# Denominators of the last pair of heads in the latent attention, summed on all 64 rows of a head and inverted without a transfer

## The chip, the cores and the metric

The kernel runs on one NeuronCore of one Trainium2 chip. Its engines work side by side, each through its own list of instructions in order: TensorE (PE) multiplies matrices and writes to PSUM, VectorE (DVE) and ScalarE (ACT) work element by element, GpSimd (POOL) does so too, and SyncE (SP) issues the transfers between DRAM and the on-chip memory SBUF. The metric is the device time of one execution in microseconds; the median of three runs counts.

## The reference, cut to what matters

Two layers of a diffusion trunk are computed for 128 context tokens and 1024 latent tokens. The second layer is a latent attention with 16 heads, each with a value of 64 columns. Latent tokens read all latent and all context keys (1152), context tokens only the context keys (128); the heads' output is multiplied by a gate and projected.

```python
def dense_attention(q, k, v, scale, sink=None):
    ...
            p = jax.nn.softmax(s, axis=-1)
        return jnp.einsum("bhgqk,bkhd->bqhgd", p.astype(v.dtype), v)

def mla_attend(q, k, v, g, w_out):
    b, L = q.shape[0], q.shape[1]
    out = dense_attention(q[:, :, :, None, :], k, v, MLA_SCALE)
    return (out.reshape(b, L, MLA_WIDTH) * jax.nn.silu(g)) @ w_out
...
        xl = xl + gate * out
    y_sample = rms_norm(xl, final_norm_w)
```

## The kernel before, in words

**Pairs and chunks.** The heads are taken in eight pairs (`pair_main`, j = 0 to 7). A pair keeps its values transposed: 128 partitions, 64 for each head, and the tokens along the row. Its tokens are worked in three chunks: latent tokens 0 to 511, latent tokens 512 to 1023, and the 128 context tokens. The last pair takes them in the order 0, context, 512.

**One chunk.** For every block of 128 keys and each of the two heads PE computes scores in three matmuls (`sc`, L1450 to L1452; operands are split into a high and a low part to keep the precision), ACT takes the exponential (L1457) into a tile `pf`, and PE multiplies the values by it into the accumulator `acco` (L1471), two key blocks at a time. A round is thus twelve score matmuls and then the value matmuls. The score buffers in PSUM are two; PE waits for the exponential that frees one. POOL adds the exponentials of all key blocks into `totals` (L1486), one tile for each head, with the keys along the partitions.

**Denominators.** `gather` runs when a chunk's values are complete. ACT copies `acco` to the pair's tile `op` (L1495). In `sums`, PE multiplies `totals` by a column of ones into `den` (L1502): one row for head 0, one for head 64 partitions further down. `store` lets ACT copy the two rows to SBUF (L1508), writes them to DRAM (`rd1_d`, shown as `rd_d`, L1509), and reads them back spread over 128 partitions, eight numbers each. `invert` takes the reciprocal on VectorE and writes it to DRAM (L1517). `fetch` loads the gate (`g1_d`, shown as `g_d`, L1523) and reads every head's reciprocals back, broadcast to its 64 partitions; their product is taken on VectorE. `gated` multiplies by `op` and stores the result to `o1_d` (shown as `o_d`, L1531). Calls made through a helper that keeps the program's order appear as L1272. `after(n, ...)` and `steps.behind(n, ...)` put these parts n steps later into the program's text.

**The output projection.** After the last pair, nine token tiles of 128 are projected. A tile's `o_d` columns of all eight pairs are loaded (L1654), so its load waits for the last pair's store of that chunk. ACT casts it to the high part, VectorE forms the low part (L249, L250, forms 128x1024), and PE runs 2 x 24 matmuls (L256 to L258) into two accumulators. VectorE multiplies an accumulator by the layer's gate (L1060), POOL adds it to the residual (L1061), then comes the final norm.

```python
            for q in range(2):
                acc = psum("mm", "acc")
                for k in range(KT):
                    mm3(acc, at[:, 0, k], at[:, 1, k], *wos[q, k], k == 0, k == KT - 1)
```

**What sets the order.** The framework orders each engine's instructions by a simulated timeline, within the dependencies and the orders that the program pins. Work of the projection therefore stands between score groups of the last chunk where the simulated timeline found its operand ready. The weights of the projection are loaded and split during the last pair.

Of the kernel before, what the change touches and what calls it, by code (L numbers as in the profile page):

```python
# [12 lines left out]
F32 = mybir.dt.float32  # L13
F32R = mybir.dt.float32r
AF = mybir.ActivationFunctionType
ALU = mybir.AluOpType
# [176 lines left out]
class Steps:  # L193
# [5 lines left out]
    def after(self, n, f, *a):  # L199
        self.due.setdefault(self.now + n, []).append(partial(f, *a))  # L200
# [20 lines left out]
def hybrid_trunk(ctx: ExitStack, tc: tile.TileContext, I, O, dbg=None, stage=99):  # L221
    nc = tc.nc
    pe, act, dve, pool, dma = nc.tensor, nc.scalar, nc.vector, nc.gpsimd, nc.sync
# [15 lines left out]
    def scratch(name, shape):  # L239
        return dr.tile(shape, F32, tag=name, name=name)  # L240

    def psum(tag, name):
        return ps.tile([128, 512], F32, tag=tag, name=name, bufs=2)
# [44 lines left out]
    g1_d = scratch("g1_d", [KT, 128, T])  # L288
    o1_d = scratch("o1_d", [KT, 128, T])
# [964 lines left out]
    p7, p7a = Space(mem), Space(mem, right=True)  # L1254
    AK, BK, AQ, BQ = [], [], [], []

    def operand_set():
# [5 lines left out]
        pool.memset(AK[i][96:97].bitcast(F32), 1.0)  # L1263
        dma.dma_start(AK[i][64:96].bitcast(F32), kp_d[0])
        dma.dma_start(BK[i][64:96].bitcast(F32), kp_d[1])
    ones = p7.tile([128, 1], F32, name="ones")
    pool.memset(ones, 1.0)
    steps = Steps()

    def pinned(f, *a):  # L1270

        tc.keep_in_program_order(f(*a))  # L1272
    after = steps.after
    either, taken = cycle(("mm", "tr")), []

    def spare(name):

        taken.append(steps.now)
        assert taken.count(steps.now) <= 4
        return psum(next(either), name)  # L1280
# [208 lines left out]

    ending = []  # L1490

    def gather(j, op, q0, n, acc, totals):

        qs = slice(q0, q0 + n)
        act.copy(op[:, qs], acc)  # L1495
        dn = p7.tile([128, 8], F32, tag="dn1", name="dn1", bufs=3)[:, 0:n // 64]
        flat = [rd1_d[2 * j + a, qs].rearrange("(p c) -> p c", p=64) for a in range(2)]

        def sums():
            den = spare("den")  # L1500
            for a in range(2):
                pe.matmul(den[a * 64:a * 64 + 1, 0:n], ones, totals[a], start=True, stop=True)  # L1502
            after(1, store, den)

        def store(den):
            row = p7.tile([65, 512], F32, tag="dr1", name="dr1", bufs=2)[:, 0:n]
            for a in range(2):
                act.copy(row[a * 64:a * 64 + 1], den[a * 64:a * 64 + 1, 0:n])  # L1508
                dma.dma_start(rd1_d[2 * j + a:2 * j + a + 1, qs], row[a * 64:a * 64 + 1])  # L1509
            for a in range(2):  # L1510
                after(2, pinned, dma.dma_start, dn[a * 64:(a + 1) * 64], flat[a])
            after(4, invert)

        def invert():
            pinned(dve.reciprocal, dn, dn)
            for a in range(2):
                dma.dma_start(flat[a], dn[a * 64:(a + 1) * 64])  # L1517
            after(2, fetch)

        def fetch():  # L1520
            gt = p7.tile([128, n], F32, tag=f"gt{n}", name="gt1")
            rb = p7.tile([128, n], F32, tag=f"rb{n}", name="rb1")
            dma.dma_start(gt, g1_d[j, :, qs])  # L1523
            for b in range(2):
                pinned(dma.dma_start, rb[b * 64:(b + 1) * 64], bcast_rows(rd1_d[2 * j + b, qs], 64))
            after(2, pinned, dve.tensor_tensor, gt, gt, rb, ALU.mult)
            after(3, gated, gt)

        def gated(gt):
            pinned((pool if ending else dve).tensor_tensor, gt, op[:, qs], gt, ALU.mult)  # L1530
            dma.dma_start(o1_d[j, :, qs], gt)  # L1531
        steps.behind(1, sums)

    wo1 = I["mla_w_out"][0]
# [69 lines left out]
    for pair in range(8):  # L1604
        op = p7.tile([128, T], F32, tag="op", name="op")
# [101 lines left out]
```

## Time and profile before

| | |
|---|---|
| median of three runs | 1846.62 us (1841.96 to 1848.19) |
| profiled execution, own time | 1853.15 us |
| its span, first to last instruction | 1851.1 us |
| mean granted TensorE clock | 0.955 |
| busy shares PE, DVE, ACT, POOL | 93%, 56%, 44%, 40% |
| last pair's denominators of chunk 0 done on PE | 1707.5 us |
| first matmul of the output projection | 1738.5 us |
| last matmul | 1842.8 us |

The profile is of one execution. Times in its rows are microseconds from the span's start, except the "mean ns of one" in groups. A row of the timeline is an instruction or several of one kind with the idle time of its engine before it and what ended that; a row of the chain is a piece of the chain of waits that ended last; a row of windows is a stretch with the busy time of each engine in it. Names such as `arenaF` are regions of SBUF from which the tiles are taken; `acc`, `sc`, `acco` and `den` are tiles in PSUM. What stands in "idle before" is time in which the engine waited; it costs something only where that engine sets the end.

### The profile page before, as it was taken

Reading aid. Unit: us, or ns where it says so; the run is one execution under the profiler, and the core shown is the slowest. Engines: PE = TensorE matmul, PEld = TensorE weight load, DVE = VectorE, ACT = ScalarE, POOL = GpSimd, SP = SyncE. Lnnn points to the kernel's source line nnn. Section 1 sums busy time; section 2 is a strip of 40 time slices with the busy share of each in tenths; the row PEclk is TensorE's granted clock in tenths of the full one; section 3 lists DMA queues with packets and bytes.
Section 4 is the critical chain, followed back from the end, with each engine's and each line's share of the span. In section 5 each row is a group of like instructions: output and inputs, shape, how many; then the busy total and the mean of one; then the engine's idle time right before and its main releaser. Section 6 shows DMA issues by size and latency. Waiting matters only on the chain.

```text
span 1851.1 us, 27076 instructions
## 1 busy us (share of the span) xinstructions
PE 1720.0 (93%) x9031; PEld 1322.7 (71%) x9031; DVE 1041.7 (56%) x1989; ACT 817.7 (44%) x1873; POOL 744.3 (40%) x741
## 2 busy tenths in 40 slices
PE   6899999999998888988999999999999999998898
PEld 3799999877775776666688898655665665654486
DVE  5665545655545467667765434655665665564243
ACT  5532323665655344444434322534535634545321
POOL 3510000133333344565624010556666665565432
PEclk9999999999998888898999999989999998999899
DMA  7423323444435697555553533010220121114342
GB/s 259 124 84 92 118 64 110 130 114 122 121 93 146 195 279 245 164 194 165 164 171 86 175 99 97 18 54 23 51 72 23 45 75 28 37 29 122 108 154 91
DMA packets 210655, 210.26 MB, mean 114 GB/s; under 512 B 36162, under 2 KB 175504, under 8 KB 210516
## 3 DMA queue, kind: packets, MB, share of 16 engines
q1 hardware_dynamic: 210372, 208.40, 37.7%
q8 instruction: 72, 1.18, 0.3%
q14 instruction: 67, 0.55, 0.1%
q0 software_dynamic: 144, 0.13, 0.0%
HBM read 151.94 MB, written 51.72 MB: 110 GB/s over the span
## 4 chain that ended last, share of the span: by engine, by line
PE 65%; DMA 12%; DVE 8%; POOL 4%; issue 3%; ACT 3%; SPq 2%; POOLq 0%; DVEq 0%; ACTq 0%
PE acc L256 12%; PE acc L258 12%; PE acc L257 12%; PE acco L1471 6%; PE pp L1429 3%; PE sc L1450 3%; DMA arenaG<-cum_d 3%; PE sc L1452 3%; PE sc L1451 3%; DVE arenaR L250 2%; DMA arenaF<-rd_d 2%; DMA rd_d<-arenaF 2%; PE st L808 1%; DMA arenaG<-rd_d 1%; PE den L1502 1%
## 5 line engine op out<-in xcount | busy, mean ns | idle before, releaser
L256 PE MATMUL acc<-arenaR 128*128 128x384 f32 (+4 forms) x1248 | 430.8, 346 | 25.5 <-ACT arenaR L249 10.4
L1486 POOL TENSOR_TENSOR arenaG<-arenaG 128x512 f32<-128x512 f32 x256 | 333.1, 1320 | 229.1 <-ACT arenaG L1457 202.0
L257 PE MATMUL acc<-arenaR 128*128 128x384 f32 (+3 forms) x1176 | 400.7, 341 | 0.1
L258 PE MATMUL acc<-arenaR 128*128 128x384 f32 (+4 forms) x1152 | 389.1, 339 | 0.2
L256 PEld LDWEIGHTS acc<-arenaR 128*128 128x128 f32 x1248 | 242.8, 195 | 69.0 <-issue 16.5
L1457 ACT ACTIVATE arenaG<-sc 128x512 f32<-128x512 f32 (+1 forms) x304 | 174.6, 580 | 218.9 <-PE sc L1452 210.9
L209 DVE TENSOR_REDUCE arenaF<-pp 128x1 f32<-128x384 f32 (+1 forms) x400 | 199.2, 539 | 110.0 <-PE pp L1429 108.6
L257 PEld LDWEIGHTS acc<-arenaR 128*128 128x128 f32 x1176 | 228.5, 194 | 15.8 <-issue 3.6
L258 PEld LDWEIGHTS acc<-arenaR 128*128 128x128 f32 x1152 | 224.0, 194 | 16.6 <-issue 2.2
L250 DVE TENSOR_TENSOR arenaR<-arenaF,arenaR 128x512 fp32r<-128x512 f32 (+2 forms) x144 | 129.7, 914 | 71.8 <-ACT arenaR L249 65.6
L249 ACT CAST arenaR<-arenaF 128x512 fp32r<-128x512 f32 (+3 forms) x160 | 101.1, 648 | 142.9 <-DMA arenaF<-in_ab_w_in_dram 24.0
L1471 PE MATMUL acco<-arenaG 128*64 128x512 f32 (+1 forms) x608 | 150.4, 609 | 0.0
L1005 ACT ACTIVATE arenaG<-arenaG,arenaF 128x128 f32<-128x128 f32 x288 | 88.4, 389 | 116.2 <-POOL arenaG L1003 115.8
L749 POOL TENSOR_TENSOR arenaG<-arenaF,arenaG 128x512 fp32r<-128x512 f32 x28 | 48.1, 1716 | 149.4 <-PE acco L753 85.6
L1429 PE MATMUL pp<-arenaR 96*128 96x384 f32 (+1 forms) x300 | 92.4, 363 | 11.6 <-DVE arenaF L209 11.1
L1450 PE MATMUL sc<-arenaR 96*128 96x512 f32 (+1 forms) x228 | 94.5, 414 | 5.5 <-ACT arenaG L1457 5.2
L1429 PEld LDWEIGHTS pp<-arenaR 96*128 96x128 f32 x300 | 55.1, 192 | 55.4 <-DVE arenaF L209 25.0
L258 PE MATMUL acc<-arenaR,arenaS 128*128 128x512 f32 (+1 forms) x240 | 91.5, 386 | 0.0
L1452 PE MATMUL sc<-arenaR 97*128 97x512 f32 (+1 forms) x228 | 89.6, 396 | 0.0
L1451 PE MATMUL sc<-arenaR 96*128 96x512 f32 (+1 forms) x228 | 89.5, 393 | 0.0
L1003 POOL TENSOR_SCALAR_AFFINE_SELECT arenaG<-arenaG 128x512 f32<-128x512 f32 x72 | 60.5, 862 | 66.4 <-DMA arenaG<-cum_d 53.9
L1471 PEld LDWEIGHTS acco<-arenaG 128*64 128x64 f32 x608 | 36.8, 140 | 70.3 <-issue 67.9
(328 smaller groups left out, 3342.8 us busy)
## 6 DMA issues: line engine op xcount, KB each, us to landing
arenaF<-in_ada_w_dram SPq DMA_DIRECT2D x96, 256.0 KB
arenaG<-cum_d SPq DMA_DIRECT2D x36, 512.0 KB
arenaF<-in_ab_w_in_dram SPq DMA_DIRECT2D x51, 256.0 KB
z_d<-arenaF SPq DMA_DIRECT2D x36, 128.0 KB
xs_d<-arenaF SPq DMA_DIRECT2D x8, 576.0 KB
arenaF<-xs_d SPq DMA_DIRECT2D x9, 512.0 KB
arenaF<-z_d SPq DMA_DIRECT2D x9, 512.0 KB
x_d<-arenaG SPq DMA_DIRECT2D x9, 512.0 KB
```

Of the source, the lines that this page charges most:

```text
L209: f()
L250: lo_eng.tensor_tensor(lo, src, hi.bitcast(F32), ALU.subtract)
L256: pe.matmul(out, ah, bh, start=first, stop=False)
L257: pe.matmul(out, ah, bl, start=False, stop=False)
L258: pe.matmul(out, al, bh, start=False, stop=last)
L1429: pe.matmul(pp[:, 0:w], AQ[s][0:96, t * 128:(t + 1) * 128], AK[s][0:96, k0:k0 + w], start=True, stop=True)
L1450: pe.matmul(sc[:, 0:n], AK[s][0:96, ks], BQ[s][:, qs], start=True, stop=False)
L1451: pe.matmul(sc[:, 0:n], BK[s][:, ks], AQ[s][0:96, qs], start=False, stop=False)
L1452: pe.matmul(sc[:, 0:n], AK[s][:, ks], AQ[s][:, qs], start=False, stop=True)
L1457: act.activation(pf, sc[:, 0:n], AF.Exp, scale=SCALE_M)
L1471: put = lambda: pe.matmul(acc[0][a * 64:(a + 1) * 64], V[:, a], pfs[a], start=(i < 2 and k < 2), stop=(last and k >= len(todo) - 2))
L1486: pool.tensor_tensor(totals[a], first[a] if i == 1 else totals[a], pfs[a], ALU.add)
```

## The change

For the last pair alone (j = 7), `gather` hands over to `gather_last`. The tile of ones becomes 64 columns wide, so that the matmul writes the denominator to all 64 rows of its head at once. VectorE takes the reciprocal of that PSUM tile, 128 x n numbers, into SBUF. The gate is loaded early and multiplied by `op`, then by the reciprocal, both on VectorE, and the product is stored. Copies of the rows on ACT and the way through `rd1_d` fall away for this pair: eight transfers in each of the three chunks. The other seven pairs keep their way and use one column of the ones.

```diff
-    ones = p7.tile([128, 1], F32, name="ones")
+    ones = p7.tile([128, 64], F32, name="ones")
...
+    def gather_last(j, op, q0, n, totals):
+
+        qs = slice(q0, q0 + n)
+        gt = p7.tile([128, n], F32, tag=f"gt{n}", name="gt1")
+        rb = p7.tile([128, n], F32, tag=f"rb{n}", name="rb1")
+        dma.dma_start(gt, g1_d[j, :, qs])
+
+        def sums():
+            den = spare("den")
+            for a in range(2):
+                pe.matmul(den[a * 64:(a + 1) * 64, 0:n], ones, totals[a], start=True, stop=True)
+            dve.tensor_tensor(gt, op[:, qs], gt, ALU.mult)
+            after(1, divided, den)
+
+        def divided(den):
+            dve.reciprocal(rb, den[:, 0:n])
+            dve.tensor_tensor(gt, gt, rb, ALU.mult)
+            dma.dma_start(o1_d[j, :, qs], gt)
+        steps.behind(1, sums)
+
     def gather(j, op, q0, n, acc, totals):
 
         qs = slice(q0, q0 + n)
         act.copy(op[:, qs], acc)
+        if j == 7:
+            return gather_last(j, op, q0, n, totals)
...
-                pe.matmul(den[a * 64:a * 64 + 1, 0:n], ones, totals[a], start=True, stop=True)
+                pe.matmul(den[a * 64:a * 64 + 1, 0:n], ones[:, 0:1], totals[a], start=True, stop=True)
```

The framework's order moves with it. On PE, in the last chunk of the last pair, the first matmuls of the output projection (`acc`) stood behind all scores:

```order
L1450 MATMUL sc<-arenaS,arenaR 128x512
L1451 MATMUL sc<-arenaS,arenaR 128x512
L1452 MATMUL sc<-arenaS,arenaR 128x512
L1471 MATMUL acco<-arenaG 64x512 x4
L256 MATMUL acc<-arenaR 128x512
L257 MATMUL acc<-arenaR 128x512
```

With the change they stand in the third of the four rounds, behind nine of its twelve score matmuls:

```order
L1450 MATMUL sc<-arenaR 128x512
L1451 MATMUL sc<-arenaR 128x512
L1452 MATMUL sc<-arenaR 128x512
L256 MATMUL acc<-arenaR 128x512
L257 MATMUL acc<-arenaR 128x512
...
L1450 MATMUL sc<-arenaS,arenaR 128x512
L1451 MATMUL sc<-arenaS,arenaR 128x512
L1452 MATMUL sc<-arenaS,arenaR 128x512
L1471 MATMUL acco<-arenaG 64x512 x4
```

Four projection matmuls moved ahead of fifteen scores, and most of tile 0's others follow between the remaining score groups.

On ACT, from the copy of the context chunk's accumulator on, the exponentials (L1457) and the casts of the first projection tiles (128x1024) stood thus:

```order
L1495 COPY arenaF<-acco 128x128
L1508 COPY arenaF<-den 1x512 x2
L1508 COPY arenaF<-den 1x128 x2
L1457 ACTIVATE arenaG<-sc 128x512 x15
L249 CAST arenaR<-arenaF 128x1024
L1457 ACTIVATE arenaG<-sc 128x512
L249 CAST arenaR<-arenaF 128x1024
```

Now:

```order
L1515 COPY arenaF<-acco 128x128
L1457 ACTIVATE arenaG<-sc 128x512 x9
L249 CAST arenaR<-arenaF 128x1024
L1457 ACTIVATE arenaG<-sc 128x512 x4
L249 CAST arenaR<-arenaF 128x1024
L1457 ACTIVATE arenaG<-sc 128x512
L249 CAST arenaR<-arenaF 128x1024
```

The four copies of denominators are gone, and the first cast stands ahead of seven exponentials instead of one.

On VectorE the reciprocals of the context chunk and of chunk 0 now stand like this, between the splits of weights (128x512) and of projection tiles (128x1024):

```order
L250 TENSOR_TENSOR arenaR<-arenaF,arenaR 128x512
L1503 TENSOR_TENSOR arenaF<-arenaF 128x512
...
L1507 RECIPROCAL arenaF<-den 128x128
L1507 RECIPROCAL arenaF<-den 128x512
L1503 TENSOR_TENSOR arenaF<-arenaF 128x128
L1508 TENSOR_TENSOR arenaF<-arenaF 128x512
L1508 TENSOR_TENSOR arenaF<-arenaF 128x128
L250 TENSOR_TENSOR arenaR<-arenaF,arenaR 128x1024 x2
```

The small reciprocal goes first and the product that is stored for chunk 0 (L1508, 128x512) is the fourth instruction behind the weights. (Of L1503 to L1515 the numbers are the changed kernel's.)

## The prediction

> **What bounds the kernel now.** I read the page first, then the end of the program by windows, then the PE timeline of the gap found there, then the chain of waits through it.
>
> The page's first part, all engines over the span:
>
> ```profile
> PE 1720.0 (93%) x9031; PEld 1322.7 (71%) x9031; DVE 1041.7 (56%) x1989; ACT 817.7 (44%) x1873; POOL 744.3 (40%) x741
> ```
>
> PE is the bound, so the change is worth what it takes out of PE's lost time, and it touches only the last pair (from about 1700 us on). Windows there; the columns are busy time by engine, then the granted clock (PEclk), the DMA share and GB/s:
>
> ```profile
> 1708.00:1712.00 4.00, 2.38 (x7) 1.37 (x8) 1.03 (x2) 3.89 (x10) 0.42 (x1) 0.96 0.50 114
> 1712.00:1716.00 4.00, 4.00 (x12) 1.92 (x12) 0.00 (x0) 1.19 (x2) 4.00 (x4) 0.61 0.46 172
> 1732.00:1736.00 4.00, 0.19 (x2) 0.00 (x0) 0.14 (x1) 0.00 (x0) 1.25 (x1) 0.95 0.62 177
> 1736.00:1740.00 4.00, 1.53 (x4) 1.16 (x4) 1.23 (x1) 1.92 (x3) 0.94 (x1) 0.50 1.07 338
> 1740.00:1744.00 4.00, 4.00 (x13) 1.66 (x12) 1.23 (x1) 1.25 (x2) 0.82 (x1) 0.70 0.83 255
> ...
> 1760.00:1780.00 20.00, 20.00 (x90) 16.55 (x89) 8.44 (x9) 4.30 (x6) 8.16 (x10) 1.00 0.62 197
> ```
>
> PE loses time twice, near 1710 and at 1732 to 1738, and behind each loss it runs about 4 us at a reduced clock. From 1760 on it is full at clock 1.00. The PE timeline says what it waited for (idle time and releaser in brackets):
>
> ```profile
> 1711.55 0.69 PE L1450 MATMUL sc<-arenaR 96*128 96x512 f32 x1 [1.42 <-ACT arenaG L1457]
> ...
> 1738.47 0.79 PE L256 MATMUL acc<-arenaR 128*128 128x512 f32 x1 [6.28 <-ACT arenaR L249]
> ...
> 1755.86 0.50 PE L256 MATMUL acc<-arenaR 128*128 128x512 f32 x1 [0.84 <-DVE arenaF L1060]
> ```
>
> The 6.28 us is the first matmul of the output projection waiting for its operand. The chain of waits shows where that comes from (start, us, what; pieces in between left out):
>
> ```profile
> 1706.35 1.18 PE den L1502 x4
> ...
> 1709.74 0.43 ACT arenaF L1508
> 1710.17 4.49 DMA rd_d<-arenaF
> ...
> 1715.22 1.89 DMA arenaF<-rd_d
> ...
> 1721.53 3.70 DMA rd_d<-arenaF
> ...
> 1725.75 4.02 DMA arenaF<-rd_d
> 1729.87 1.00 DVE arenaF L1272
> ...
> 1733.03 4.32 DMA arenaF<-o_d
> 1737.37 1.05 ACT arenaR L249
> ```
>
> From the denominators' end (1706.35 + 1.18 = 1707.53) to the cast's end (1738.42) are 30.9 us. All up to the product at 1729.87 is the denominators' way through DRAM and back: four hops and the waits between them.
>
> **The change part by part.** The sum is made against the profiled execution (1853.15 us, span 1851.1); its gain in us is then taken off the median of the three runs (1846.62), which lies 6.5 us lower.
>
> *Removed on ACT.* Four copies of denominator rows stood ahead of the exponentials:
>
> ```profile
> 1709.15 1.73 ACT L1508 COPY arenaF<-den 1x512 f32<-1x512 f32 x4
> 1710.90 1.08 ACT L1457 ACTIVATE arenaG<-sc 128x512 f32<-128x512 f32 x2
> ```
>
> The exponential at 1710.90 releases the score buffer that PE waits 1.42 us for; 1.73 us earlier, there is no wait. That wait leaves PE 2.38 us busy of 4, and the clock of the next window falls to 0.61: 4.00 x (1 - 0.61) = 1.56 us. Term: **+1.42 and +1.56**, both gone.
>
> *Removed: the gap at 1732.* **+6.28**, and the low clock behind it: 1.53 x 0.50 + 4.00 x 0.30 = **+1.97**.
>
> *Moved: the tile's first evacuation.* The 0.84 us at 1755.86 is PE waiting for an accumulator that L1060 releases. In the new PE order tile 0's work lies between score groups, and L1060 has long been done when its buffer is wanted again: **+0.84**. All five losses together: 12.07 us.
>
> *Added: a shorter chain, which may still be late.* PE's new order asks for the first projection matmul nine score matmuls into the third round of the last chunk. Before, that place was reached between these two groups of three:
>
> ```profile
> 1723.47 0.50 PE L1450 MATMUL sc<-arenaR 96*128 96x512 f32 x1
> ...
> 1724.28 0.39 PE L1450 MATMUL sc<-arenaS,arenaR 96*128 96x512 f32 x1
> ```
>
> At 1724.28, then, less the 2.98 us gained above: **1721.3**. Now the new chain. Reciprocals over the whole span and products after 1640 us, in groups by shape (count | busy us, mean ns | idle before):
>
> ```profile
> L500 DVE RECIPROCAL arenaS<-arenaS 128x288 f32<-128x288 f32 x1 | 2.0, 1953 | 0.0
> L1272 DVE RECIPROCAL arenaF<-arenaF 128x8 f32<-128x8 f32 x16 | 3.1, 193 | 16.8 <-DMA arenaF<-rd_d 16.8
> ...
> L1272 DVE TENSOR_TENSOR arenaF<-arenaF 128x512 f32<-128x512 f32 x7 | 10.2, 1460 | 5.3 <-DMA arenaF<-rd_d 5.2
> L1060 DVE TENSOR_TENSOR arenaF<-acc,arenaF 128x512 f32<-128x512 f32 x16 | 11.0, 690 | 31.1 <-PE acc L258 31.1
> ```
>
> The 690 ns of the fourth row is a product that takes one input from PSUM. The reciprocal goes by elements: (1953 - 193) / 280 = 6.29 ns each, so 1.953 + 224 x 0.00629 = 3.36 us for 512 and 0.95 for 128. No reciprocal here reads PSUM; below, 3.36; above I allow half as much again (5.0), since L1060 shows no surcharge for a PSUM input. I take 3.36. A product costs 0.69 to 1.46 us; POOL's additions run beside these, so 1.46.
>
> ```profile
> 1704.99 0.33 SPq L1523 DMA_DIRECT2D arenaF<-g_d  x1
> ...
> 1708.65 0.69 DVE L250 TENSOR_TENSOR arenaR<-arenaF,arenaR 128x512 fp32r<-128x512 f32 x1 [0.31 <-ACT arenaR L249]
> ...
> 1762.16 0.35 SPq L1531 DMA_DIRECT2D o_d<-arenaF  x1
> 1764.20 1.01 SPq L1654 DMA_DIRECT2D arenaF<-o_d  x2
> ```
>
> Step by step: VectorE ends its weight split (L250) at 1709.34, some 0.3 later with the gate product in front of it (the gate is issued at 1704.99): 1709.6. Both reciprocals, the small one first: 1713.9. The context chunk's gate product, a quarter as wide, 0.5: 1714.4. The product that is stored, 1.46: 1715.9. Store to next load issue, 1764.20 - 1762.16 = 2.04: 1717.9; the gate load of the next chunk is issued between, 0.35: 1718.3. Load 4.32, cast 1.05: **1723.7**. PE stands **2.4 us** (-2.4) instead of 6.28. Bounds: with two loads in flight where there were four transfers, a load of 3.0 gives 1.1; the dearer reciprocals give 4.5.
>
> Queued behind that cast on ACT are the exponentials of the third round; behind the stored product SP holds the next gate load and the projection's loads. They lose the same 2.4 us, not a further one.
>
> *The clock behind the new wait.* A PE window 2.38 busy of 4 was followed by clock 0.61 (rows above), so a wait of 2.4 us can cost from 0 to 1.97 us; I take **-0.9**. [...]
>
> *Denominator matmuls.* Same 512 columns stream; only the weights are wider:
>
> ```profile
> L1471 PEld LDWEIGHTS acco<-arenaG 128*64 128x64 f32 x608 | 36.8, 140 | 70.3 <-issue 67.9 <-PE sc L1452 0.7 <-PE pp L1429 0.7
> L1502 PEld LDWEIGHTS den<-arenaG,arenaF 128*1 128x1 f32 x96 | 2.6, 81 | 9.2 <-issue 6.8 <-POOL arenaG L1486 2.0
> ```
>
> Twelve loads (two records to each of six matmuls) x 59 ns = 0.7 us if nothing hides it, 0 if the running matmul does; **-0.2**.
>
> *At nothing.* The last chunk's reciprocal and two products (3.36 + 1.46 + 1.46 = 6.3 us) stand on VectorE ahead of the evacuation of tile 1. PE has two accumulators, 48 matmuls, and they run at this pace:
>
> ```profile
> 1840.08 0.39 PE L258 MATMUL acc<-arenaR 128*128 128x512 f32 x1
> ...
> 1842.80 0.39 PE L258 MATMUL acc<-arenaR 128*128 128x512 f32 x1
> ```
>
> Twelve in 2.72 us, 0.227 each: 10.9 us of cover, 4.6 left; without it, each us over costs one. That chunk's chain to its load (about 15 us) lies under the rest of tiles 1 to 3, 142 x 0.227 = 32 us. The 24 removed transfers and SP's shorter queue count only through the chain. POOL loses one product (it sat idle), VectorE gains it.
>
> Sum: 12.07 - 2.4 - 0.9 - 0.2 = **8.6 us**. Profiled execution 1853.15 to 1844.6; median 1846.62 to **1838.0**.
>
> **The rivals.** *A, the chain wins:* loads near 3 us and products near 0.69 bring the cast before 1721.3. For it: fewer transfers collide. Against: POOL adds all through. Gain 12.07 - 0.2 = 11.9: 1834.7.
>
> *B, the chain is later than worked out:* with dearer reciprocals from PSUM PE waits 4.4 us, and the low clock is paid in full: 12.07 - 4.4 - 1.97 - 0.2 = 5.5, 1841.1. At its far end the wait stays 6.28 (a cast at 1727.6, 3.9 later than worked out): 12.07 - 6.28 - 1.97 - 0.2 = 3.6, 1843.0. For it: no row prices a PSUM reciprocal, and two of VectorE's products now compete with POOL's additions on the chain. Against: 0.690 us with a PSUM operand.
>
> *C, slower:* the reciprocal of PSUM costs several times 6.29 ns. The pair of 640 elements loses the whole gain once it takes 4.3 + 8.6 = 12.9 us, 20 ns an element. At 25 ns it takes 16.0: the wait grows by 11.7, the clock by 1.1 more, 8.6 - 12.8 = 4.2 us slower; and the last chunk's 12.8 + 2.9 us overrun the 10.9 of cover by 4.8. 1846.62 + 9.0 = 1855.6. Only the missing row speaks for it.
>
> That the change doesn't do what it says can be left out: the orders show the transfers gone.
>
> **How the numbers follow.** Forecast 0.52, A 0.18, B 0.25, C 0.05. What a measurement of this kernel can tell from no change is about 0.3%, 5.5 us. Faster by more: 0.47 of the forecast, A whole, 0.07 of B: 0.72. Slower by more: C and a hundredth for what no row shows: 0.06. Within: the rest, 0.22. The range takes A's end (1834.7, less some 2.5 us by which the three runs' median may lie off: 1832) and B's (1843.0 and 2: 1845); what is left out at both ends is under 0.2.
>
> **What would show it.** Right: no L1508 copies and no 1.42 us wait near 1710; clock 1.00 from 1712 to 1716; L1507 on 128x512 near 3.4 us; the first L256 of the projection at 1721 to 1725 with an idle of 1 to 4 us; last matmul some 8 us earlier. Wrong: an idle above 5 us before that L256, a reciprocal above 5 us, or PE waiting for L1060 after the last denominators.

## The result, and the profile after

The changed kernel's median is 1837.56 us (1830.42 to 1841.14, seven runs), that of the kernel before in the runs beside it 1848.19 us (1841.96 to 1853.25). The ratio is 0.994, with a 95% interval of 0.992 to 0.996: 11 us faster, between 7 and 15. The forecast was 1838.0 and "faster".

The profiled execution of the changed kernel took 1836.65 us (span 1834.9), that of before 1853.15. Not all of these 16.5 us belong to the change, so the two traces are lined up first. In both, a matmul of L1429 waits 2.77 us, some 70 us ahead of the last pair's first denominators, where the code doesn't differ. PE's timeline of the kernel before has it at

```profile
1632.80 0.44 PE L1429 MATMUL pp<-arenaR 96*128 96x384 f32 x1 [2.77 <-DVE arenaF L209]
```

and that of the changed kernel, with the two score matmuls of L1450 that waited last, the end of the denominators of chunk 0 and the context between them (1700.47 + 1.24 = 1701.71), the first projection matmul and the last one, at

```profile
1626.86 0.69 PE L1429 MATMUL pp<-arenaR 96*128 96x384 f32 x1 [2.77 <-DVE arenaF L209]
...
1697.19 0.50 PE L1450 MATMUL sc<-arenaR 96*128 96x512 f32 x1 [1.20 <-ACT arenaG L1457]
1700.47 1.24 PE L1502 MATMUL den<-arenaG,arenaF 128*64 128x128 f32 x4
1702.43 0.50 PE L1450 MATMUL sc<-arenaR 96*128 96x512 f32 x1 [0.72 <-ACT arenaG L1457]
...
1717.37 0.50 PE L256 MATMUL acc<-arenaR 128*128 128x512 f32 x1 [1.58 <-ACT arenaR L249]
...
1826.57 0.39 PE L258 MATMUL acc<-arenaR 128*128 128x512 f32 x1
```

The stretch from that L1429 to the last L258 is called the **last part** from here on. It holds 807 matmuls in every kernel for which it is given. Before it took 1842.80 - 1632.80 = 210.0 us, after 1826.57 - 1626.86 = 199.7: **10.3 us less**. Of the other 6.2 us, 5.9 lie ahead of it (1632.80 against 1626.86), and the first experiment shows that as much comes and goes without any edit.

The 6.28 us in front of the projection have become 1.58, and no wait for L1060 is left at all. The windows of the changed kernel answer those of before near 1710 and behind the projection's start (busy PE, PEld, DVE, ACT, POOL, then PEclk, DMA share, GB/s):

```profile
1708.00:1712.00 4.00, 3.94 (x16) 2.28 (x18) 1.99 (x3) 2.39 (x4) 3.53 (x3) 1.00 0.24 88
1712.00:1716.00 4.00, 3.75 (x15) 1.68 (x11) 0.00 (x0) 0.60 (x1) 3.94 (x4) 1.00 0.79 229
1716.00:1720.00 4.00, 2.63 (x11) 1.58 (x13) 1.23 (x1) 2.63 (x4) 2.23 (x3) 1.00 0.38 111
1720.00:1724.00 4.00, 4.00 (x19) 2.60 (x16) 0.00 (x0) 1.54 (x2) 3.31 (x3) 1.00 0.84 246
```

PE is nearly full up to the one wait (3.94 and 3.75 us of 4), and the clock stays at 1.00, ahead of it and behind. The chain of waits shows what the way from the denominators to the projection is now (pieces in between left out):

```profile
1703.81 0.82 DVE arenaF L1507
...
1707.81 0.28 DVE arenaF L1503
1708.09 1.73 DVE arenaF L1508 x2
1709.82 1.98 DMA o_d<-arenaF
1711.82 0.32 SPq L1497
1712.18 4.07 DMA arenaF<-o_d
1716.27 1.05 ACT arenaR L249
1717.37 0.50 PE acc L256
```

One store and one load are left where there were six hops, and the cast ends at 1717.32. The groups of the last 200 us give the price of what was added on VectorE:

```profile
L1507 DVE RECIPROCAL arenaF<-den 128x512 f32<-128x512 f32 x2 | 6.6, 3320 | 0.0
L1508 DVE TENSOR_TENSOR arenaF<-arenaF 128x512 f32<-128x512 f32 x2 | 2.5, 1233 | 0.0
L1507 DVE RECIPROCAL arenaF<-den 128x128 f32<-128x128 f32 x1 | 1.0, 951 | 0.0
```

The reciprocal that reads PSUM takes 3.32 us for 512 numbers a row and 0.95 for 128, as worked out from those that read SBUF (3.36 and 0.95).

### The profile page after: what moved, and what is told of

The parts are those of the page before. It is cut to its first block, busy times and chain, and to the rows that moved or that the text cites. A ratio compares the mean times of both kernels' runs of the same rounds, so it can differ in the third digit from the quotient of the medians.

```text
span 1834.9 us, 27025 instructions
## 1 busy us (share of the span) xinstructions
PE 1712.0 (93%) x9031; PEld 1317.3 (72%) x9031; DVE 1049.5 (57%) x1990; ACT 815.3 (44%) x1867; POOL 741.5 (40%) x740
## 4 chain that ended last, share of the span: by engine, by line
PE 41%; DMA 11%; DVE 7%; issue 3%; POOL 3%; ACT 2%; SPq 2%; POOLq 0%; DVEq 0%; ACTq 0%
PE acc L256 7%; PE acc L258 6%; PE acc L257 6%; PE acco L1471 6%; PE pp L1429 3%; PE sc L1450 3%; PE sc L1452 3%; PE sc L1451 3%; DMA arenaG<-cum_d 2%; DMA arenaG<-rd_d 2%; DVE arenaR L250 2%; DMA arenaF<-rd_d 1%; DMA rd_d<-arenaF 1%; PE yacc L1011 1%; POOL arenaG L1003 1%
## 5 line engine op out<-in xcount | busy, mean ns | idle before, releaser
L258 PE MATMUL acc<-arenaR 128*128 128x384 f32 (+4 forms) x1152 | 387.6, 338 | 0.2
L1457 ACT ACTIVATE arenaG<-sc 128x512 f32<-128x512 f32 (+1 forms) x304 | 174.7, 580 | 222.7 <-PE sc L1452 214.7
L258 PEld LDWEIGHTS acc<-arenaR 128*128 128x128 f32 x1152 | 222.6, 193 | 16.5 <-issue 3.8
L1429 PE MATMUL pp<-arenaR 96*128 96x384 f32 (+1 forms) x300 | 92.7, 365 | 10.9 <-DVE arenaF L209 10.4
L1450 PE MATMUL sc<-arenaR 96*128 96x512 f32 (+1 forms) x228 | 94.1, 413 | 4.4 <-ACT arenaG L1457 4.0
L1429 PEld LDWEIGHTS pp<-arenaR 96*128 96x128 f32 x300 | 55.0, 192 | 55.1 <-DVE arenaF L209 23.9
L258 PE MATMUL acc<-arenaR,arenaS 128*128 128x512 f32 (+1 forms) x240 | 90.7, 383 | 0.0
```

Of the source, the lines that this page charges most:

```text
L258: pe.matmul(out, al, bh, start=False, stop=last)
L1429: pe.matmul(pp[:, 0:w], AQ[s][0:96, t * 128:(t + 1) * 128], AK[s][0:96, k0:k0 + w], start=True, stop=True)
L1450: pe.matmul(sc[:, 0:n], AK[s][0:96, ks], BQ[s][:, qs], start=True, stop=False)
L1457: act.activation(pf, sc[:, 0:n], AF.Exp, scale=SCALE_M)
```

## The experiments

All kernels are compared by their last part, which holds every place that the edits touch, and by their time. In the table, the first wait is PE's idle time in front of the first projection matmul, the evacuation wait its idle time for L1060, and low clock the stretches at half clock that began behind 1695 us. For all eight pairs no last part is given, since L1429 waits differently there. All but the last column is read from one execution of each kernel; each ratio is against runs of the kernel before that were made beside that kernel's own.

| kernel | last part | first wait | evacuation wait | low clock | median, ratio to before (95%) |
|---|---|---|---|---|---|
| before | 210.0 | 6.28 | 0.84 | 3.4 + 6.8 | |
| before once more | 209.1 | 5.16 | 0.84 | 3.4 + 6.8 | 1846.14 (one run) |
| after | 199.7 | 1.58 | none | none | 1837.56, 0.994 (0.992 to 0.996) |
| new way for chunk 0 only | 207.2 | 3.34 | 3.07 | 6.8 + 3.4 | 1846.28, 1.0015 (0.9995 to 1.0035) |
| for all but chunk 0 | 205.1 | 2.51 | none | 3.4 | 1838.40, 0.9966 (0.9944 to 0.9987) |
| first tiles don't need the last pair | 207.6 | none | 3.23 | 6.8 + 3.4 | 1845.58, 1.000 (0.998 to 1.002) |
| rows copied by VectorE | 207.9 | 8.48 | none | 10.2 | 1845.80, 0.9994 (0.9977 to 1.0012) |
| reciprocals four times | 208.4 | 6.10 | none | 6.8 | 1843.33, 0.9985 (0.9967 to 1.0003) |
| first tile first | 198.3 | 0.71 | none | none | 1835.29, 0.9934 (0.991 to 0.9957) |
| chunk 0 only, evacuation first | 207.4 | 4.64 | 2.10 | 3.4 + 3.4 | 1848.12, 1.0001 (0.9981 to 1.0022) |
| chunk 0 only, rows kept | 208.7 | 6.28 | none | 10.2 | 1847.53, 0.9996 (0.998 to 1.0013) |
| all but the last chunk | 204.7 | 1.82 | 3.23 | 3.4 | 1843.06, 0.9971 (0.995 to 0.9992) |
| all but the last chunk, rows kept | 200.9 | 0.23 | none | 3.4 | 1839.05, 0.9962 (0.9941 to 0.9983) |
| all eight pairs | | 0.32 | none | none | 1832.93, 0.9927 (0.990 to 0.9955) |

How much low clock falls into a last part is partly chance, as the last section shows. Ahead of 1695 us it is three pieces of 3.41 us in ten of the thirteen executions with a last part, and four in "for all but chunk 0", "reciprocals four times" and "chunk 0 only, rows kept", whose last parts are up to 1.7 us longer by that alone. With half of PE's busy time in the low pieces taken off, the last parts are 201.4 and 199.5 us for the two executions of before, 194.7 after, 197.6 for chunk 0 only, 199.4 with its rows kept, 198.0 for all but the last chunk, and 194.4 with its rows kept.

### The kernel before, once more

No edit.

> The kernel before, unchanged, profiled once more, to see what in a trace differs without any edit. The stretch meant in all expectations: from the end of the second pair of denominator matmuls of the last pair of heads to the start of the last projection matmul. Before 135.27 us (1707.53 to 1842.80), after 124.86 us (1701.71 to 1826.57). The trace of after is already 5.8 us ahead at the start of the stretch, where the code does not differ. Theory T (the change acts only inside the stretch; what lies ahead differs because the clock falls in other places from execution to execution): the stretch is 135 within 1 us with the same waits of 1.4 and 6.3 us, and its start lies somewhere else by several us, as the low clock ahead of it does. Rival R0 (the 5.8 us belong to the change): the start lies within 1 us of 1707.5.

PE's timeline of this execution:

```profile
1626.72 0.45 PE L1429 MATMUL pp<-arenaR 96*128 96x384 f32 x1 [2.77 <-DVE arenaF L209]
...
1835.79 0.39 PE L258 MATMUL acc<-arenaR 128*128 128x512 f32 x1
```

The stretch of the expectation came out at 135.06 us, the last part at 209.1. The wait in front of the projection was 5.16 us, where 6.3 was expected, so a first wait can differ by 1 us without any edit. The last part begins at 1626.72, six microseconds ahead of the first execution of the same kernel and level with the changed one (1626.86). Rival R0 falls: what lies ahead of the last part is not the change's.

### The new way for chunk 0 alone

```diff
-        if j == 7:
+        if j == 7 and q0 == 0 and n == 512:
             return gather_last(j, op, q0, n, totals)
```

> The new way for one chunk of the last pair alone, the first 512 tokens, on which the first projection matmuls wait; the context chunk and the second chunk go the old way through DRAM. Theory T (only what is late at the first projection matmul costs, so one chunk carries the gain): the four row copies on ScalarE are gone for this chunk (two narrow ones of the context remain, some 0.3 us each), the wait at the first projection matmul is 0 to 3 us, the stretch 125 to 127 us, gain 8 to 10 us of the 10.4. Rival R1 (the gain goes with the transfers taken out, 24 in all, of which this leaves 16): the stretch is near 132, gain 3 to 4 us.

```profile
1718.07 0.80 PE L256 MATMUL acc<-arenaR 128*128 128x512 f32 x1 [3.34 <-ACT arenaR L249]
...
1743.30 0.51 PE L256 MATMUL acc<-arenaR 128*128 128x512 f32 x1 [3.07 <-DVE arenaF L1060]
```

These rows of PE's timeline show why the kernel gained next to nothing (stretch 132.7, last part 207.2, ratio 1.0015). The first wait is 3.34 us, not 1.58, and a wait of 3.07 us for the first evacuation has come up, which neither kernel had in that size; low clock follows both. The stretch is R1's 132, but the trace shows two places, not a price for every transfer. Theory T, that the one chunk the projection waits for carries the gain, falls.

### All but chunk 0

```diff
-        if j == 7:
+        if j == 7 and q0 > 0:
             return gather_last(j, op, q0, n, totals)
```

> The new way for the context chunk and the second chunk of the last pair, the old way for the first 512 tokens. Theory T: the chain through DRAM of the first chunk stays as it was, and PE waits 5 to 6.5 us at the first projection matmul again, with the low clock behind it; two of the four row copies on ScalarE are gone, so the 1.42 us wait in front shrinks to about 0.7 to 1; stretch 133 to 135, gain 0 to 2 us. Rival R1 (the gain goes with the transfers taken out, 16 of 24): stretch near 128, gain some 7 us.

```profile
1730.89 0.53 PE L256 MATMUL acc<-arenaR 128*128 128x512 f32 x1 [2.51 <-ACT arenaR L249]
```

Chunk 0 goes through DRAM as before, and still the first wait falls to 2.51 us and the stretch to 128.1: another miss for T, near R1's 128. Its chain, with every hop it had, takes 25.0 us from the denominators' end to the projection (1705.87 to 1730.89) against 29.9 and 30.9 in the two executions of before. The two chains of waits show what became shorter. From the store of chunk 0's reciprocals to the landing of their broadcast it is 5.0 us here (1715.75 to 1720.78) and 12.3 in the kernel before (1717.43 to 1729.77), where a hop of the context chunk stands between the two. So the chunks that the projection does not wait for were part of the price, and the question became by which way.

### The first four tiles without the last pair

```diff
-            dma.dma_start(raw, o1_d[:, :, tok].rearrange("k p n -> p k n"))
+            if t < 4:
+                dma.dma_start(raw[:, 0:7], o1_d[0:7, :, tok].rearrange("k p n -> p k n"))
+                dma.dma_start(raw[:, 7:8], o1_d[6:7, :, tok].rearrange("k p n -> p k n"))
+            else:
+                dma.dma_start(raw, o1_d[:, :, tok].rearrange("k p n -> p k n"))
```

> The kernel before, with the projection's first four token tiles reading the seventh pair of heads twice and the last pair not at all: those tiles leave the last pair's contribution out, and so do not wait for it. The same number of bytes and matmuls; the chain of denominators through DRAM runs on as before. Theory T (the chain costs only because the first projection matmul waits for it): the wait of 6.28 us, the low clock behind it (1.97) and the 0.84 us at L1060 go, 1.42 and 1.56 in front stay or are covered by projection work: stretch 123 to 127. Rival R1 (transfers, copies and SyncE's queue cost by themselves): the stretch stays above 131.

```profile
1697.23 0.79 PE L1450 MATMUL sc<-arenaR 96*128 96x512 f32 x1 [2.86 <-ACT arenaG L1457]
...
1744.25 0.50 PE L256 MATMUL acc<-arenaR 128*128 128x512 f32 x1 [3.23 <-DVE arenaF L1060]
```

The long wait is gone and little is gained (last part 207.6; the stretch can't be compared, since projection work moved ahead of its start). A cast of the projection's weights, which waits on ACT until 1696.38 for its transfer, now stands ahead of an exponential; PE waits 2.86 us for that from 1694 on, with 6.8 us of low clock behind it, and the evacuation wait is there again, 3.23 us. As a test of the chain it is inconclusive; it shows the second wait in another kernel that starts the projection early and keeps the way through DRAM.

### The rows copied by VectorE

```diff
-                act.copy(row[a * 64:a * 64 + 1], den[a * 64:a * 64 + 1, 0:n])
+                (dve.tensor_copy if j == 7 else act.copy)(row[a * 64:a * 64 + 1], den[a * 64:a * 64 + 1, 0:n])
```

> The kernel before with the last pair's denominator rows copied by VectorE in place of ScalarE; the way through DRAM and back stays whole. Theory T2 (PE's waits count, and the longest chain at the first projection matmul stays): the 1.42 us wait in front and the low clock behind it go, PE reaches the first projection matmul earlier and waits longer there (6 to 9 us in place of 5.2 to 6.3), with low clock behind; last part 207 to 210 us against 209.1 to 210.0, gain 0 to 2. Rival R2 (the copies on ScalarE are what costs): last part 205 to 206.5, the 3 us in front gained in full.

```profile
1734.55 0.80 PE L256 MATMUL acc<-arenaR 128*128 128x512 f32 x1 [8.48 <-ACT arenaR L249]
```

The 1.42 us in front are gone as the copies leave ACT, and the first wait grows by 2 to 3 us: 207.9 us, as T2 had it. Ridding ACT of the four copies gains 1 to 2 us of the last part, and nothing that shows in the time (0.9994), while the chain behind them stays.

### Each reciprocal four times

```diff
-            dve.reciprocal(rb, den[:, 0:n])
+            for _ in range(4):
+                dve.reciprocal(rb, den[:, 0:n])
```

> The kernel after with each reciprocal done four times over (12.8 us more on VectorE between the denominators and the first projection matmul, 10 more for the last chunk). The scheduler then puts the projection behind all scores of the last chunk. Theory T2 (only what exceeds PE's other work costs): cast some 28.4 us after the denominators, PE there after some 22: a wait of 5 to 7 us and a low clock behind it, last part 206 to 210 against 199.7. Rival R1 (the chain's length counts us for us): 212 or more. Rival R3 (the gain is the removed transfers and copies, VectorE's time is free): 199 to 202.

```profile
1740.83 0.80 PE L256 MATMUL acc<-arenaR 128*128 128x512 f32 x1 [6.10 <-ACT arenaR L249]
```

12.8 us more on the chain cost 8.7 us of the last part (208.4 against 199.7, up to 1.7 of them the low clock ahead of 1695), inside T2's 206 to 210. The framework put the projection behind all scores, and PE's other work swallowed the rest. The length of the chain counts where it exceeds that work; time on VectorE is not free (R3), and it isn't paid us for us (R1).

### The first tile first

```diff
-            after(1, divided, den)
+            if q0 == 0:
+                after(1, divided, den, 0, 128)
+                after(3, divided, den, 128, 512)
+            else:
+                after(3 if n == 128 else 1, divided, den, 0, n)
...
-        def divided(den):
-            dve.reciprocal(rb, den[:, 0:n])
+        def divided(den, lo, hi):
+            pinned(dve.reciprocal, rb[:, lo:hi], den[:, lo:hi])
```

The product and the store are cut in the same way.

> The kernel after with the first chunk's reciprocal, product and store cut into 128 and 384 columns, so that the first token tile is stored and loaded ahead of the rest, and the context's reciprocal behind them. Theory T2 (the remaining 1.58 us of wait at the first projection matmul is the chain through reciprocal, product, store and load): chain some 2 us shorter, the wait 0 to 0.5, last part 198 to 199 against 199.7. Rival (the remaining wait is not the chain's but the order of ScalarE's queue, or the shifted order of projection work brings back the wait for the evacuation): 199.5 to 203.

```profile
1717.18 0.50 PE L256 MATMUL acc<-arenaR 128*128 128x512 f32 x1 [0.71 <-ACT arenaR L249]
```

The last part is 198.3 us, 1.4 less than after; the wait, 0.71, is a little above the 0.5 expected. In the time this can't be told apart from after (0.9934 against 0.994).

### Chunk 0 alone, with the evacuation put first

```diff
-                residual(p, q, acc, x, gate, pool if t < NT - 1 else dve)
+                tmp = residual(p, q, acc, x, gate, pool if t < NT - 1 else dve)
+                if (t, q) == (0, 0):
+                    zero = p.tile([128, 1], F32, tag="z8", name="z8", bufs=1)
+                    dve.tensor_tensor(zero, tmp[:, 0:1], tmp[:, 0:1], ALU.subtract)
...
-            split(at[:, 0], at[:, 1], raw)
+            if t == 3:
+                act.activation(at[:, 0], raw, AF.Identity, bias=zero)
+                dve.tensor_tensor(at[:, 1], raw, at[:, 0].bitcast(F32), ALU.subtract)
+            else:
+                split(at[:, 0], at[:, 1], raw)
```

> Since the runs differ by several us before the last part begins, all kernels are measured from the start of the line-1429 matmul that waits 2.77 us (the same wait in every trace) to the start of the last projection matmul, called the last part: before 210.0 us, the kernel before once more 209.1, after 199.7, first chunk only 207.2, all but the first chunk 205.1, first tiles free 207.6. The new-way-for-the-first-chunk kernel got a wait that the kernel after does not have: 3.07 us for the first evacuation (L1060), which stands on VectorE behind the split of the fourth token tile, whose cast stands on ScalarE behind two row copies that wait for the last denominators; 3.41 us of low clock follow. This run is that kernel with the fourth tile's cast made to wait for the first evacuation (a bias of zero computed from it), so that the scheduler must put the evacuation ahead of that split. Nothing else is changed, and the row copies and transfers stay. Theory T2 (the gain needs both waits gone, the one at the first projection matmul and the one at the first evacuation): the 3.07 us fall to 0 to 0.5, the low clock behind goes, last part 202 to 203.5, 4 to 5 us faster than first chunk only. Rival R1 (the remaining 16 transfers and the row copies cost by themselves): last part 206 to 208.

The evacuation in VectorE's timeline, and the piece ahead of it in the chain of waits:

```profile
1750.33 0.69 DVE L1060 TENSOR_TENSOR arenaF<-acc,arenaF 128x512 f32<-128x512 f32 x1 [10.65 <-DMA rd_d<-arenaF]
```

```profile
1749.09 1.12 DMA rd_d<-arenaF
```

L1060 now stands ahead of the fourth tile's split, VectorE is idle, and it still waits: for the transfer that writes the last chunk's rows to DRAM. 2.10 of the 3.07 us stay, and the last part, 207.4 us, lies in R1's range. T2's account by queue order falls, and the row suggests another, which the next run tests: the output of L1060 lies in the region `arenaF`, on memory that held those rows, and may not be written until they have been read. (The first wait of this execution was longer too, 4.64 us; more on that below.)

### Chunk 0 alone, with the rows' memory kept

```diff
-    p7.drop(*[k for k in p7.rings if k[:2] not in ("op", "gt", "rb")])
+    p7.drop(*[k for k in p7.rings if k[:2] not in ("op", "gt", "rb", "dr", "dn")])
```

The buffers of the rows (`dr`) and of their reciprocals (`dn`) are no longer handed on to the projection.

> In the two kernels where the projection starts early and the last chunk still goes through DRAM (first chunk only; evacuation first), the first evacuation L1060 waits until the store of the last chunk's row copies is done (releaser: the transfer rd_d<-arenaF), whatever its place in VectorE's queue: its output buffer lies on the memory that held those rows. This run is the new way for the first chunk only, with the buffers of rows and reciprocals kept apart from the projection's buffers (they are not handed back), so that the evacuation no longer overlays them. Theory T3 (memory handed from the rows to the evacuation's output is the second wait): no PE wait for L1060 above 0.5 us, the 3.41 us of low clock behind it gone, the wait at the first projection matmul stays 3 to 4.6 us with its low clock; last part 202 to 204 against 207.2 and 207.4, total 3 to 5 us faster than those two. Rival R4 (the second wait is one of queue order on ScalarE and VectorE only): the wait for L1060 stays 2 to 3 us, last part 206 to 208.

PE's first wait, then the store of chunk 0 (L1509) and the first tile's load (L1676) in SP's queue, then the chain of waits up to that load (pieces in between left out):

```profile
1726.33 0.79 PE L256 MATMUL acc<-arenaR 128*128 128x512 f32 x1 [6.28 <-ACT arenaR L249]
```

```profile
1712.78 0.59 SPq L1509 DMA_DIRECT2D o_d<-arenaF  x1
...
1720.96 1.21 SPq L1676 DMA_DIRECT2D arenaF<-o_d  x2
```

```profile
1707.71 0.27 ACT arenaF L1530
...
1708.00 3.63 DMA rd_d<-arenaF
...
1714.39 5.41 DMA rd_d<-arenaF
1719.82 0.46 SPq L1272
```

The evacuation wait is gone altogether, so T3's mechanism for it holds and R4 falls. But the last part is 208.7, not 202 to 204: the first wait went to 6.28 us with 10.2 us of low clock. The rows say why the cast is late. Chunk 0's product is ready and its store issued at 1712.78, and its load is issued only at 1720.96, 8.2 us later, because SP's queue holds the context chunk's broadcast (L1272) ahead of it, and that waits for the context's own hop through DRAM. The chain of waits runs through the context chunk's row copy (L1530) and its two stores to `rd_d`, not through chunk 0's product. With chunk 0 alone it was much the same (7.6 us from store to load), and the cast ends only 0.9 us later behind the denominators here (19.7 against 18.8). That the wait grew by 2.9 us is mostly the framework's doing: it asks for the projection 2.1 us earlier, in the same place as in after.

### All but the last chunk

```diff
-        if j == 7:
+        if j == 7 and q0 != 512:
```

> The new way for the first and the context chunk, the old way for the last chunk alone. Theory T3 (two places: what stands in front of the first tile's load on SyncE's queue sets the wait at the first projection matmul, the last chunk's rows set the wait for the first evacuation): without the context's transfers in the queue the first wait is 1.5 to 2 us as in the kernel after, the wait for L1060 2 to 3.1 us as in first chunk only, with 3.41 us of low clock behind it; last part 203 to 205, between after (199.7) and first chunk only (207.2). Rival R1 (time goes with the number of transfers, 8 of 24 left): 202 to 203 with no such wait. Rival R5 (the last chunk's way is hidden, as the prediction had it for the new one): 199 to 200.5.

PE's timeline, and the chain of waits up to the first evacuation (pieces in between left out):

```profile
1725.08 0.50 PE L256 MATMUL acc<-arenaR 128*128 128x512 f32 x1 [1.82 <-ACT arenaR L249]
...
1750.40 0.50 PE L256 MATMUL acc<-arenaR 128*128 128x512 f32 x1 [3.23 <-DVE arenaF L1060]
```

```profile
1746.22 0.96 PE den L1524 x2
...
1747.80 0.58 ACT arenaF L1530
...
1748.40 1.13 DMA rd_d<-arenaF
...
1749.65 0.70 DVE arenaF L1060
```

With the context's hops gone the first wait is 1.82 us; with the last chunk's rows back the evacuation wait is 3.23 (a little above the 3.1 expected), and 3.41 us of low clock follow it. Last part 204.7, as T3 had it. The chain reads like a list of the mechanism: denominators, row copies on ACT, their store, and only then the evacuation. Against chunk 0 alone, PE's idle time in the last part is nearly the same (9.6 and 9.8 us); it is the low clock that takes 2.9 us less. By the time the run does gain on chunk 0 alone (0.9971 against 1.0015). The context chunk's row copies and products change together with its transfers here, so it is the chain of the run before that points to the queue place.

### All but the last chunk, with the rows' memory kept

Both edits above together.

> The two cures together: the new way for the first and the context chunk (wait at the first projection matmul 1.82 us in that run, 6.28 where the context's transfers were left on SyncE's queue), and the rows of the last chunk, which still goes through DRAM, kept off the memory of the evacuation's output (which left no wait for L1060 at all). Theory T3 (just these two places make the gain; the last chunk's own way through DRAM is hidden): first wait 1 to 2.5 us, no wait for L1060, no or one piece of low clock (3.41 us) after 1700 us, last part 199.5 to 202 against 199.7 after, though eight of the 24 transfers and two of the four wide row copies are still there. Rival R1 (time goes with the transfers left): 202.5 or more. Rival R5 (the two cures get into each other's way through the scheduler's order, a third wait comes): 203 to 208.

SP's queue, the first projection matmul, and the first two evacuations:

```profile
1712.74 0.80 SPq L1509 DMA_DIRECT2D o_d<-arenaF  x2
...
1715.10 6.80 SPq L1676 DMA_DIRECT2D arenaF<-o_d  x3
```

```profile
1720.25 0.50 PE L256 MATMUL acc<-arenaR 128*128 128x512 f32 x1 [0.23 <-ACT arenaR L249]
```

```profile
1732.05 0.68 DVE L1060 TENSOR_TENSOR arenaF<-acc,arenaF 128x512 f32<-128x512 f32 x1
...
1740.41 0.69 DVE L1060 TENSOR_TENSOR arenaG<-acc,arenaF 128x512 f32<-128x512 f32 x1 [5.84 <-PE acc L258]
```

PE's work behind the denominators of chunk 0 stands in the same order, matmul for matmul, as in the run with 6.28 us of wait and as in after. So the new order on PE is not what makes the gain: with it, the last part is 208.7, 200.9 or 199.7 us. The store is issued at 1712.74, and the load now follows 2.4 us behind it; the first wait is 0.23 us, less than expected. The first evacuation runs at 1732.05, ahead of the last chunk's denominators (1738.69), without idle time before it; the second writes to another region (`arenaG`) and waits for nothing but its matmuls. The last part is 200.9 us, within 1.2 us of after, though the last chunk still takes its eight transfers and two wide row copies. A piece of low clock, behind a 1.76 us wait for exponentials ahead of the projection, accounts for the rest: without low clock it is 194.4 us against 194.7. R5 falls, and R1 by 1.6 us of this one execution. The time (0.9962) lies with after, the intervals overlapping, but as near to all but the last chunk (0.9971), so the times do not show that the second cure adds to the first.

### The new way for all eight pairs

```diff
-        if j == 7:
+        if True:
```

> The new way for all eight pairs: 7 more pairs with some 7.6 us of reciprocals each and wider products on VectorE (about 50 us more there between 1240 and 1700 us, where it is 59% busy), and 168 transfers and 42 copies on ScalarE gone. Theory T3 (a chain through DRAM costs only where TensorE waits for its end; for the earlier pairs it has a pair's time, some 58 us, before anything needs it): nothing gained in the stage, last part 199 to 201 as after, total within 3 us of after. Rival R6 (copies and transfers cost by themselves): several us faster than after. Rival R7 (VectorE's longer queue delays the maxima of line 209, for which TensorE already waits 9.8 us in the stage): slower than after by 3 us or more.

```profile
PE 1711.0 (94%) x9031; PEld 1315.9 (72%) x9031; DVE 1081.5 (59%) x1990; ACT 797.4 (44%) x1825; POOL 739.7 (40%) x740
```

```profile
1713.41 0.50 PE L256 MATMUL acc<-arenaR 128*128 128x512 f32 x1 [0.32 <-ACT arenaR L249]
```

VectorE's busy time rises by 32 us against after and the time does not (0.9927 against 0.994, a difference of 2.4 us with intervals that overlap widely). R7 falls; R6 and T3 can't be told apart by it. It has the lowest median of all, 1832.93 us, but whether it beats after is open.

## Why the prediction was right

The kernel became faster, as forecast, and the forecast was 0.4 us off the median. Part of that closeness is luck: by the ratio the gain is 11 us, by the last part 10.3, and 8.6 were predicted; the runs of before beside the changed kernel had a median 1.6 us above the three that the forecast started from.

**The five losses (12.07 us).** All five are gone as the prediction had them: no 1.42 us near 1710, clock 1.00 behind it, no 6.28, no low clock behind that, no 0.84. With the new wait taken off, 12.07 - 1.58 = 10.49 us against 10.3 measured. The 0.2 between is the size that the wider weight loads were given, and the traces' groups of instructions show the denominator matmuls 0.17 us longer in all (605 ns against 592 for each of eight, 286 against 270 for each of four). In these two traces PE's idle time in the last part fell by 7.0 us and what the low clock took by 3.6, so about a third of the gain is clock, which is partly chance.

**The new wait (2.4 predicted, 1.58 measured).** PE stood there 1717.37 - 1.58 - 1701.71 = 14.1 us behind the denominators, 13.8 predicted; the cast ended 15.6 us behind them, 16.2 predicted. Reciprocals, gap from store to load (2.36 us against 2.04 + 0.35), load (4.07 against 4.32) and cast fit. The one term that was short is the stored product. The two products of 512 in the groups above take 2 x 1.233 = 2.47 us; the last chunk's takes 0.69, so chunk 0's took 1.78, where 1.46 was taken. The last chunk's product in VectorE's timeline of after, and what POOL did meanwhile:

```profile
1744.49 0.69 DVE L1508 TENSOR_TENSOR arenaF<-arenaF 128x512 f32<-128x512 f32 x1
```

```profile
1745.81 0.19 POOL L391 TENSOR_SCALAR arenaF<-arenaF 128x1 f32<-128x1 f32 x1 [6.25 <-ACT arenaF L1690]
```

The same instruction takes 0.69 us while POOL sits idle (6.25 us up to 1745.81), and 1.78 in the window 1708 to 1712, where POOL is busy 3.53 of 4. The product with the gate at 1702.52, of the same form and with POOL idle too (7.40 us up to 1704.19), takes 0.68. That POOL's additions make it longer is a reading of these rows alone: no run here takes them away.

**The low clock behind it (0.9 predicted, nothing measured).** The bounds were 0 and 1.97, and the lower one came. The last section shows that this was close to a coin's toss.

**The reciprocal from PSUM.** 3.32 us where 3.36 was taken; rivals B and C rested on a surcharge that these rows do not show. Rival A falls too: the cast was not ahead of PE.

**The step that failed** is the one that priced edits at nothing: "The 24 removed transfers and SP's shorter queue count only through the chain", with the evacuation's 0.84 us put down to the new order on PE ("L1060 has long been done"). The runs show two ways by which the other two chunks count. The first does go through chunk 0's chain, but hangs on another chunk's edit: the context chunk's broadcast stands in SP's queue ahead of the first tile's load and holds it until its own hop is done, 8.2 us from store to load where 2.4 suffice. The second does not go through that chain at all: the last chunk's rows occupy the memory of the evacuation's output, and with the projection started early, PE waits 3.1 to 3.2 us for it in three kernels, plus some low clock. So the reordering does not by itself remove the wait for L1060; kept on the old way, the last chunk makes it larger than it was. The sum came out right since the change takes all three chunks at once. Of the 10.3 us, chunk 0's edit alone brings 2 to 3 in the last part.

What stays open: why chunk 0's edit alone, which shortens the last part by 2 to 3 us, shows nothing in the time (1.0015, 0.9995 to 1.0035); how much of the gain in time each of the two cures brings, since the last parts are of one execution each; and whether all eight pairs or the first tile first gain anything over after.

## What to carry to other kernels

In this kernel PE's waits were held by what stood ahead of a load in the issuing queue (8.2 us from store to load, 2.4 without it) and by a buffer whose memory a neighbour inherited (3.1 to 3.2 us). So price a removed chain with the queue places and the memory that it frees, not only with its own length. When a partial change gains nothing, look for the second wait: here, low clock aside, the last part gained nothing from either of two cures alone, and all that was missing from both together. Line up two traces at a wait that no edit touches before subtracting their times.

## What was unexpected of the hardware

The low clock comes in pieces of 3.41 us at 0.50, or two to four of them in a row (6.83 us from 1735.58 on before, 13.65 from 691.46 on after). They lie on a grid: between 1630 and 1740 us those of the kernel before begin at 1633.18, 1674.14, 1711.69 and 1735.58, 12, 11 and 7 times 3.413 us apart. Whether a piece comes goes with how busy PE was in the 3.41 us ahead of it; no long gap is needed: the longest in the first of the stretches below is 1.42 us. Windows of the kernel before, laid on these pieces:

```profile
1708.28:1711.69 3.41, 1.95 (x7) 0.99 (x8) 0.75 (x2) 3.31 (x9) 0.12 (x1) 1.00 0.48 113
1711.69:1715.11 3.42, 3.42 (x8) 1.89 (x10) 0.00 (x0) 1.49 (x3) 3.42 (x3) 0.50 0.62 218
```

and of the changed kernel:

```profile
1715.46:1718.87 3.41, 1.82 (x9) 1.24 (x7) 1.23 (x1) 2.03 (x3) 1.64 (x2) 1.00 0.55 164
1718.87:1722.29 3.42, 3.42 (x15) 1.54 (x14) 0.00 (x0) 0.77 (x2) 3.31 (x3) 1.00 0.67 163
```

In the first, 1.95 us busy of 3.41 are followed by a piece at 0.50; in the second, 1.82 of 3.41 are not. So between half and 70% busy it can go either way. Counted over six traces (before, before once more, after, chunk 0 only, first tile first, all pairs; from 300 us on, pieces at full clock), the next piece was low in 92 of 94 cases where PE had been busy less than half of it, in 17 of 32 at 50 to 60%, in 20 of 70 at 60 to 70%, 10 of 86 at 70 to 80%, 1 of 97 at 80 to 90% and in none of 2057 above. Where a wait falls on this grid differs from execution to execution: the 2.77 us of L1429 ended 0.38 us ahead of the start of a low piece before (1632.80 and 1633.18) and 0.15 behind it after (1626.86 and 1626.71), with 3.41 us of low clock in the one and 6.83 in the other. So a wait of some 1.5 us costs nothing beside itself (1.58 after) or, by estimate, half of 3.41, 1.7 us, more (1.42 before). That the kernel before ran between 1837.0 and 1852.6 us in 27 runs fits this; no run here shows that the clock is all of that spread.
